# Input projections of heads 2 to 7 as block products, seven for eight

## The chip, the cores and the metric

The kernel runs on one core of a Trainium2 chip. The metric is the device time of one execution in microseconds (us). Five engines work side by side, each in the order of its own queue: TensorE (PE: matmuls, with its weight loads, PEld), VectorE (DVE: elementwise work and sums), ScalarE (ACT: functions, copies, rounding), GpSimd (POOL) and SyncE (SP), whose queue here issues the DMA transfers. They wait for one another by semaphores. SBUF is the memory that the engines work in, PSUM the one that TensorE writes its sums to.

## The reference

One step of a one-layer encoder for 512 prompt frames and 32 frames of a running stream, 544 tokens of 2048 features. The part that matters here is the first projection and the recurrent heads that read it:

```python
def token_mixer(x, s0, ...):
    proj = x @ w_in                                  # 544 x 2048 by 2048 x 4928
    hq, hf, hi, hg, cq, ckv, kr = jnp.split(proj, SPLITS, axis=-1)
    f = lb + (1.0 - lb) * jax.nn.sigmoid(hf)
    o_h, s_new = hgrn2_recurrence(heads(hq), heads(1.0 - f), heads(jnp.log(f)), heads(hi), s0, blk)
    o_h = rms_norm(o_h, hgrn_norm_g) * jax.nn.silu(hg)
    ...                                              # latent attention from cq, ckv, kr gives o_a
    out = jnp.concatenate([o_h, o_a], axis=-1) @ w_out
```

Each of the eight recurrent heads needs four blocks of 128 columns of the projection: q, f (forget gate), i (input) and g (output gate). Behind it stand the output projection, a layer norm and a feed-forward part with a convolution. All is float32.

## The kernel before

**Matmuls.** Features lie on the 128 partitions and tokens along the free axis. A float32 product is made from three matmuls in a faster rounded format (`mm3`, line 111): each operand is split into a rounded part and its remainder (`aH`, `aL` for the inputs; `wh`, `wl` for the weights), and rounded by rounded, rounded weight by remainder and remainder weight by rounded are summed in PSUM. ACT makes the rounded part of a weight (line 104), DVE the remainder (line 105). A matmul takes 128 features by 128 columns and one half of the tokens, 272, so one block of 128 columns costs 16 feature blocks x 3 x 2 halves = 96 matmuls.

**Heads.** `head_qf(h)` (line 338) projects q and f of a head, `head_ig(h)` (line 348) i and g: two blocks of 128 columns, 192 matmuls, from four weight pieces of 512 KB (`piece`: a load into one of three `raw` tiles, then the split into one of four pairs `wh`, `wl`). When a block is done, ACT copies it out of PSUM or applies the sigmoid, and DVE scales the forget gate (line 345) or multiplies the output gate (line 355).

**The recurrence** of a head runs beside the projections of the next: `levels(h)` (line 646) combines blocks of frames of doubled length in seven levels. In each, PE multiplies `Kp` and `Qp` (lines 674 to 679), then DVE updates `Qp` (line 680), POOL updates `Kp` (line 682) and DVE puts the result into a matrix (line 692). The next level's matmuls read the updated `Qp` and `Kp`. `finish(h)` (line 701) transposes, forms the states `S` and the output (lines 740, 742), normalises it (ACT squares at line 745, DVE sums at line 748, POOL takes the power at line 750, DVE multiplies at line 752), transposes it back (line 758) and multiplies by the gate (line 760). Outputs go to DRAM (`cat_dr`) for the output projection, whose first pieces (`out_first`, line 778) read them back into tiles `cx` and split them.

**Order.** `weave` (line 155) writes a chain of small steps between the pieces of a projection, at a given ratio; from that text a scheduler lays down the final queue of every engine. On the chip each queue is then worked off in order. The feed-forward part, written by hand, has its products in the form that the change brings to the heads.

Of the kernel before, what the change touches and what calls it, by code (L numbers as in the profile page):

```python
# [7 lines left out]
F32 = mybir.dt.float32  # L8
R = mybir.dt.float32r
# [6 lines left out]
P = 128  # L16
# [36 lines left out]
MANUAL = {mybir.EngineType.PE, mybir.EngineType.DVE, mybir.EngineType.Activation}  # L53
LEVELS = [1, 2, 4, 8, 16, 32, 64]


@with_exitstack
def tile_encoder_step(ctx, tc, xp, xs, w_in, w_kr, w_q_b, w_kv_b, w_out, w_up, w_gate, w_down, w_down2,
                      par_d, latp_d, krp_d, st_d, ident_d, cos_d, sin_d, amask_d, hmask_d,
                      y_d, lat_d, kr_d, stp_d, sts_d, conv_d):  # L60
    nc = tc.nc
# [46 lines left out]
    def piece(src, kc, ncols):  # L108
        return split_w(load_raw(src, kc, ncols), kc, ncols)
# [68 lines left out]

    ALLK = list(range(KD))

    def in_pieces(c):
        return lambda kk: piece(w_in[kk, c], 4, 256)

    aH, aL = [], []

# [7 lines left out]
    with tc.tile_pool(name="p0", bufs=1) as p0, tc.tile_pool(name="ps0", bufs=4, space=PSUM) as ps0:  # L193
# [12 lines left out]
        def load_first(kk):  # L206
            for g in range(2):
                raws[kk, g] = p0.tile([P, 4, 256], F32, name="raw0", tag="raw0", bufs=1) if g else \
                    wp.tile([P, 1024], F32, name="raw", tag="raw", bufs=3).rearrange("p (k c) -> p k c", k=4)
                dma(raws[kk, g], w_in[kk, 16 + g].rearrange("p (k c) -> p k c", k=4))  # L210

        G.memset(xt[4], 0.0)
        load_x(0)
# [413 lines left out]
        return cH[k], cL[k]  # L627


    with tc.tile_pool(name="gp", bufs=1) as gp, tc.tile_pool(name="psg", bufs=1, space=PSUM) as psg:  # L630
        hm = gp.tile([P, T + 272 * 6], I32, name="hm")
        dma(hm, hmask_d)
# [3 lines left out]
        rec = {}  # L636
        kT = gp.tile([P, 5, P], F32, name="kT")
        G.memset(kT[:, 4], 0.0)

        def sw_tile():  # L640
            return psg.tile([P, 1024], F32, name="sw", tag="sw")
# [59 lines left out]
        def finish(h):  # L701
            v, gate = hi[h], hgate[h]
            Kp, Qp, tot, tots, at, s0 = rec[h]
            vT = gp.tile([P, 5, P], F32, name="vT", tag="vT", bufs=1)
            for src, dst in ((Kp, kT), (v, vT)):
                tp = sw_tile()
                for j, (a, b) in enumerate(TOK):
                    PE.transpose(tp[:, j * P:(j + 1) * P], src[:, a:b], ident)  # L708
                if dst is kT:
                    A.activation(kT[:, :4].rearrange("p j c -> p (j c)"), tp[:, :512], AF.Copy)  # L710
                    A.activation(kT[96:128, 4], tp[96:128, 512:640], AF.Copy)
                else:
                    A.activation(dst.rearrange("p j c -> p (j c)"), tp[:, :640], AF.Copy)
                yield
            yield
            ss = s1_tile()
            for c in range(4):
                PE.matmul(ss[:, c * P:(c + 1) * P], kT[:, c], vT[:, c], start=True, stop=True)  # L718
            S = [None]
            for c in range(4):  # L720
                sc = gp.tile([P, P], F32, name="S", tag="S", bufs=5)
                if c == 0:
                    V.tensor_copy(sc, ss[:, 0:P])
# [7 lines left out]
            s1o = gp.tile([P, P], F32, name="s1o", tag="s1o", bufs=2)  # L731
            V.scalar_tensor_tensor(out=s1o, in0=s0, scalar=tots[:, 16:17], in1=ss[:, :P], op0=ALU.mult, op1=ALU.add)
            dma(sts_d[h], s1o)
            yield
            yield
            ops_ = sw_tile()
            for c, (ta, tb) in enumerate(TOK):
                cs = slice(c * P, (c + 1) * P)
                st = S[c] if c < 4 else s0
                PE.matmul(ops_[:, cs], at[:, ta:tb], vT[:, c], start=True, stop=c == 0)  # L740
                if c:
                    PE.matmul(ops_[:, cs], Qp[:, ta:tb], st, start=False, stop=True)  # L742
            o3 = ops_[:, :640].rearrange("p (c v) -> p c v", c=5)
            sq = gp.tile([P, 5, P], F32, name="sqg", tag="sqg", bufs=1)
            A.activation(sq, o3, AF.Square)
            r0 = gp.tile([P, 5], F32, name="r0", tag="r0", bufs=2)
            r1 = gp.tile([P, 5], F32, name="r1", tag="r1", bufs=2)
            V.reduce_sum(out=r0, in_=sq, axis=AX.X)
            V.tensor_scalar(out=r0, in0=r0, scalar1=1.0 / P, scalar2=RMS_EPS, op0=ALU.mult, op1=ALU.add)
            G.tensor_tensor(out=r1, in0=r0, in1=nhalf, op=ALU.pow)  # L750
            on = gp.tile([P, 5, P], F32, name="on", tag="on", bufs=1)
            V.tensor_tensor(out=on, in0=o3, in1=r1[:, :, None].to_broadcast([P, 5, P]), op=ALU.mult)
# [6 lines left out]
            o = gp.tile([P, T], F32, name="og", tag="og", bufs=2)  # L759
# [12 lines left out]
        for h in range(2, HEADS):  # L772
            weave([head_ig(h)], [levels(h)], 0.6)
            if h < HEADS - 1:
                weave([head_qf(h + 1)], [finish(h)], 0.7)
        wo_tiles = [main_tile(), main_tile()]

        def out_first():
            for kk in range(4):
                for k in CAT_ORDER[4 * kk:4 * kk + 4]:  # L780
                    if k != HEADS - 1:
                        cx = gp.tile([P, T], F32, name="cx", tag="cx", bufs=4)
                        dma(cx, cat_dr[k // 2][:, k % 2, :])
                        cH[k], cL[k] = split_act(cx)
            fin = finish(HEADS - 1)
            ks = CAT_ORDER
            for kk in range(4):
                wh, wl = out_piece(ks[kk * 4] // 4, 0)
                if kk == 3:
                    run(fin)  # L790
                for t, ps in enumerate(wo_tiles):
                    for k in range(4):
                        kg = ks[kk * 4 + k]
                        mm3(both(ps), (wh[:, k], wl[:, k]), (t * P, t * P + P), cact(kg),
                            kk == 0 and k == 0, kk == 3 and k == 3)
                        if k % 2 and kk < 3:
                            next(fin, None)
# [124 lines left out]
    hid_dr = dram.tile([P, NF - FD, T], F32, name="hd", tag="hd")  # L922

    ORDER = ("11", "s1", "s2", "s4", "s3", "12", "22")
    STORED = ("11", "12", "s1", "s2", "s3", "22", "s4")
    home, x1_op = {}, {}

# [1051 lines left out]
def _arrays(i):  # L1982
# [16 lines left out]
    w_main = np.concatenate([w_h, w_in[:, 4096:4864]], axis=1)  # L1999
# [10 lines left out]
    def striped(w):  # L2010
# [2 lines left out]
        return w.reshape(c // 512, 2, 2, P, 2 * NS * P)  # L2013

    arrs = [("xp", i["x_prompt"][0]), ("xs", i["x_sample"][0]), ("w_in", pieces(w_main, 4, 256)),
            ("w_kr", pieces(w_in[:, 4864:], 8, 64)[:, 0]), ("w_q_b", pieces(i["w_q_b"][0], 2, 384)),
            ("w_kv_b", pieces(i["w_kv_b"][0], 2, 512)), ("w_out", pieces(i["w_out"][0], 4, 256)),
            ("w_up", quads(i["w_ffn_up"][0])), ("w_gate", quads(i["w_ffn_gate"][0])),
# [30 lines left out]
```

## Time and profile before

| what | us |
|---|---|
| median of three timed runs (2419.14 to 2421.63) | 2420.24 |
| the profiled execution, its own time | 2417.4 |
| its span, first to last instruction | 2415.6 |
| up to the end of head 0's projections | 302 |
| projections of head 1 | 75 |
| projections of heads 2 to 7 | 364 |
| output projection and norm | 222 |
| feed-forward part: products up and gate, then down | 1278 |
| rest | 174 |

The stretches are read off the starts of instructions on the timeline. In the profile, the busy time of an engine counts its instructions, and overlapping matmuls count once; a group of instructions shows busy time, mean length of one, and the idle time just before them with what ended it; the chain of work that ended last is followed back from the last instruction. What a wait is put down to is inferred from semaphores.

### The profile page before, as it was taken

How to read it: one execution, taken by the hardware profiler on the slowest of the kernel's cores; microseconds unless marked ns; L12 is line 12 of the kernel's file. 1: busy time of each engine (PE TensorE's matmuls, PEld its weight loads, DVE VectorE, ACT ScalarE, POOL GpSimd, SP SyncE). 2: the span in 40 equal slices, each digit the busy share in tenths (PEclk: the TensorE clock that was granted, in tenths of full speed). 3: DMA queues.
4: the chain of work that ended last, by engine and by line, in shares of the span. 5: the costliest groups of instructions: out<-in, count | busy, mean ns of one | idle time of the engine just before them, and what ended most of it. 6: DMA issues, size and time to landing. Idle time of an engine off the chain costs nothing.

```text
span 2415.6 us, 44603 instructions
## 1 busy us (share of the span) xinstructions
PE 2365.5 (98%) x18750; PEld 2343.0 (97%) x18750; DVE 1666.5 (69%) x2263; ACT 980.0 (41%) x1487; POOL 181.6 (8%) x219
## 2 busy tenths in 40 slices
PE   7999999999999999999999999999999999999997
PEld 7999899999999998989999999999999999999996
DVE  7445544434345456889888888888777888888566
ACT  4244422222223224655555555555445433333234
POOL 4010020111111120000000000000000100000023
PEclk9999999999999999999999999999999999999998
DMA  7232132222235244536353534435243874642422
GB/s 238 89 94 71 61 103 86 78 79 78 79 92 192 88 123 150 178 119 203 109 194 110 178 130 143 165 115 192 88 126 120 344 298 139 234 134 88 121 66 75
DMA packets 123848, 324.29 MB, mean 134 GB/s; under 512 B 11008, under 2 KB 57856, under 8 KB 119040
## 3 DMA queue, kind: packets, MB, share of 16 engines
q1 hardware_dynamic: 114384, 277.99, 35.3%
q0 software_dynamic: 5040, 39.00, 4.1%
q10 hardware_dynamic: 4224, 4.46, 0.5%
q8 instruction: 147, 2.41, 0.4%
q14 instruction: 53, 0.43, 0.1%
HBM read 266.09 MB, written 53.92 MB: 132 GB/s over the span
## 4 chain that ended last, share of the span: by engine, by line
PE 80%; DVE 3%; ACT 1%; issue 1%; ACTq 0%; DVEq 0%
PE main L1025 20%; PE main L116 20%; PE acc L1025 16%; PE main L1053 8%; PE acc L1053 6%; PE acc L116 6%; PE s L676 1%; DVE wl L977 1%; PE sw L740 0%; PE sw L708 0%; ACT zb L1145 0%; ACT wh L976 0%; PE sw L742 0%; PE s L718 0%; PE sw L659 0%
## 5 line engine op out<-in xcount | busy, mean ns | idle before, releaser
L976 ACT ACTIVATE wh<-raw 128x1024 fp32r<-128x1024 f32 x340 | 359.9, 1059 | 414.0 <-DVE raw L969 133.7
L977 DVE TENSOR_TENSOR wl<-raw,wh 128x1024 fp32r<-128x1024 f32 x340 | 415.7, 1223 | 133.5 <-ACT wh L976 132.6
L116 PE MATMUL main<-aH,wh 128*128 128x272 f32 (+2 forms) x1536 | 348.5, 296 | 0.2 <-ACT x L262 0.2
L116 PE MATMUL main<-aL,wh 128*128 128x272 f32 (+2 forms) x1536 | 337.3, 289 | 3.7 <-POOL aL L264 3.7
L116 PE MATMUL main<-aH,wl 128*128 128x272 f32 (+2 forms) x1536 | 337.7, 289 | 0.0
L105 DVE TENSOR_TENSOR wl<-raw,wh 128x1024 fp32r<-128x1024 f32 (+2 forms) x128 | 149.7, 1171 | 236.1 <-ACT wh L104 231.3
L104 ACT ACTIVATE wh<-raw 128x1024 fp32r<-128x1024 f32 (+2 forms) x128 | 126.3, 991 | 364.5 <-PE main L116 284.2
L1025 PE MATMUL main<-op,wh 128*128 128x272 f32 x1408 | 265.6, 288 | 0.0
L1025 PE MATMUL acc<-ops,wh 128*128 128x272 f32 x1344 | 255.7, 289 | 4.2 <-DVE ops L1106 4.2
L116 PEld LDWEIGHTS main<-aL,wh 128*128 128x128 f32 x1536 | 249.9, 189 | 4.4 <-POOL aL L264 4.4
L1025 PE MATMUL main<-ops,wh 128*128 128x272 f32 x1344 | 254.1, 287 | 0.0
L116 PEld LDWEIGHTS main<-aH,wh 128*128 128x128 f32 x1536 | 248.6, 190 | 2.0 <-issue 0.5
L116 PEld LDWEIGHTS main<-aH,wl 128*128 128x128 f32 x1536 | 249.1, 190 | 0.0
L1025 PEld LDWEIGHTS main<-op,wh 128*128 128x128 f32 x1408 | 221.0, 188 | 0.0
L1025 PEld LDWEIGHTS acc<-ops,wh 128*128 128x128 f32 x1344 | 212.3, 189 | 4.5 <-DVE ops L1106 4.5
L1025 PEld LDWEIGHTS main<-ops,wh 128*128 128x128 f32 x1344 | 211.0, 188 | 0.0
L1025 PE MATMUL main<-op,wl 128*128 128x272 f32 x704 | 203.1, 289 | 0.9 <-DVE wl L977 0.9
L1025 PE MATMUL acc<-ops,wl 128*128 128x272 f32 x672 | 194.4, 289 | 0.0
L1025 PE MATMUL main<-ops,wl 128*128 128x272 f32 x672 | 193.8, 288 | 0.2 <-DVE wl L977 0.2
L1025 PE MATMUL acc<-op,wh 128*128 128x272 f32 x832 | 158.9, 289 | 1.6 <-DVE eg L1249 1.6
L976 ACT ACTIVATE wh<-rawl 128x1024 fp32r<-128x1024 f32 x93 | 98.5, 1059 | 105.9 <-DVE rawl L969 41.8
L969 DVE TENSOR_TENSOR raw<-raw,raw 128x1024 f32<-128x1024 f32 x114 | 139.2, 1221 | 1.7 <-DMA raw<-in_w_up 0.2
(395 smaller groups left out, 4865.7 us busy)
## 6 DMA issues: line engine op xcount, KB each, us to landing
raw<-in_w_in SPq DMA_DIRECT2D x76, 512.0 KB, 3.6
raw<-in_w_up SPq DMA_DIRECT2D x72, 512.0 KB, 4.6
raw<-in_w_gate SPq DMA_DIRECT2D x72, 512.0 KB, 4.2
raw<-in_w_down SPq DMA_DIRECT2D x71, 512.0 KB, 3.8
raw<-in_w_out SPq DMA_DIRECT2D x40, 512.0 KB, 3.5
opd<-ohl SPq DMA_DIRECT2D x16, 1088.0 KB, 5.5
ops<-opd POOLq DMA_DIRECT2D x16, 1088.0 KB, 9.2
opd<-ohl SPq DMA_DIRECT2D x16, 816.0 KB, 6.4
```

The costliest lines, as they stand in the source:

```text
L104: A.activation(dst(hv), src(rv), AF.Copy)
L105: V.tensor_tensor(out=dst(lv), in0=src(rv), in1=dst(hv).bitcast(F32), op=ALU.subtract)
L116: PE.matmul(ps, ww[:, wcols[0]:wcols[1]], aa[:, hs[j]], start=first and i == 0, stop=last and i == 2, skip_group_check=True)
L676: PE.matmul(ps[:, j * 64:(j + 1) * 64], Kp[:, a:b], Qv[:, j * bt:(j + 1) * bt, 1, :], start=True, stop=True)
L969: V.tensor_tensor(out=out, in0=a, in1=b, op=ALU.subtract)
L976: A.activation(wh, src, AF.Copy)
L977: V.tensor_tensor(out=wl, in0=src, in1=wh.bitcast(F32), op=ALU.subtract)
L1025: PE.matmul(ps, ww[:, k * P:(k + 1) * P], aa, start=self.first and k == 0 and i == 0, stop=k == n - 1 and i == 2, skip_group_check=True)
L1053: PE.matmul(banks[:, 512 * u:512 * u + NI], ww[:, (u * n + k) * P:(u * n + k + 1) * P], aa, start=self.first and k == 0 and i == 0, stop=k ...
```

## The change

The projections of heads 2 to 7 (twelve groups: q with f, i with g) are made as a two by two block product: inputs in two halves of 1024 features, tokens in two halves of 272, outputs in the two blocks of 128 columns. Eight block products become seven, on sums and differences of blocks, in the order `11, s1, s2, s4, s3, 12, 22`. Each product is 8 feature blocks x 3 = 24 matmuls of 272 columns. The weights of a group come as four blocks of 512 KB (two halves of inputs by two of outputs). DVE forms differences of them in place (`form`), and each of the seven is split as before (`split`). The sums of inputs `s1`, `s2`, `s4` are formed once, beside head 1, from the stored inputs (`h0_dr`), into tiles of their own; the fourth, `s3`, goes to DRAM and from there over the first 1024 features of the second half of tokens in `aH` and `aL`, which nothing reads after head 1. Products accumulate in two PSUM halves; four results are copied out by ACT, three added by DVE. Head 0 and 1 and the attention's projections stay as they were.

```diff
+N_PLAIN = 4
...
+        sums = {n: [gp.tile([P, 2, 4, NI], R, name=f"{n}{i}", tag=f"{n}{i}") for i in range(2)] for n in ("s1", "s2", "s4")}
...
+        def load_sums():
+            for k in range(HK):
+                for dst, kg, j in (("s1", k, 1), ("s2", k, 0), ("s4", HK + k, 0)):
+                    dma(part(dst, k, 1).bitcast(F32), h0_dr[kg][:, H_[j]])
+                dma(part("s1", k, 0).bitcast(F32), h0_dr[HK + k][:, H_[1]])
+
+        def sums_of_inputs():
+            load_sums()
+            for k in range(HK):
...
+                V.tensor_tensor(out=a, in0=t0, in1=t1, op=ALU.subtract)
+                V.tensor_tensor(out=b, in0=t1, in1=t1b, op=ALU.add)
+                V.tensor_tensor(out=c, in0=b, in1=t0, op=ALU.subtract)
+                two(a, s3[:, 0], s3[:, 1])
+                dma(s3_dr[k], s3.bitcast(F32))
+                yield
+                V.tensor_tensor(out=a, in0=t0b, in1=c, op=ALU.subtract)
+                for n, x in (("s1", b), ("s2", c), ("s4", a)):
+                    two(x, part(n, k, 0), part(n, k, 1))
+                yield
+
+        def place_s3():
+            for k in range(HK):
+                for i, t in enumerate((aH, aL)):
+                    dma(t[k][:, H_[1]].bitcast(F32), s3_dr[k][:, i])
+
+        class Divided:
...
+            def form(self, name):
+                if name == "11":
+                    for key in ("11", "12", "22", "21"):
+                        self.load(key)
+                r = self.raw
+                for n, out, a, b in (("s1", "11", "12", "11"), ("s2", "11", "22", "11"), ("s3", "12", "22", "12"),
+                                     ("22", "21", "21", "11")):
+                    if n == name:
+                        V.tensor_tensor(out=r[out], in0=r[a], in1=r[b], op=ALU.subtract)
...
+        def divided(c, a, b, after):
+            ps = main_tile()
+            x, y = ps[:, :NI], ps[:, 512:512 + NI]
+            t0, t1 = H_
+            for i, name in enumerate(ORDER):
+                n = 7 * (c - N_PLAIN) + i
+                ready(n + 2)
+                wh, wl = split_of.pop(n)
+                out = x if name in ("11", "s2", "s3", "22") else y
+                for k in range(HK):
+                    oh, ol = operand(name, k)
+                    for q, (ww, aa) in enumerate(((wh, oh), (wh, ol), (wl, oh))):
+                        PE.matmul(out, ww[:, k * P:(k + 1) * P], aa, ...)
+                    if k % 4 == 3:
+                        yield
+                kept = {"11": a[:, t0], "s1": b[:, t1], "s2": b[:, t0], "22": a[:, t1]}.get(name)
+                if kept is not None:
+                    A.activation(kept, out, AF.Copy)
+                else:
+                    z = {"s4": b[:, t0], "s3": b[:, t1], "12": a[:, t0]}[name]
+                    V.tensor_tensor(out=z, in0=z, in1=out, op=ALU.add)
+                    if name != "12":
+                        after(z)
...
-                sc = gp.tile([P, P], F32, name="S", tag="S", bufs=5)
+                sc = gp.tile([P, P], F32, name="S", tag="S", bufs=4)
...
-            on = gp.tile([P, 5, P], F32, name="on", tag="on", bufs=1)
+            on = sq
...
-        weave([head_qf(1)], [levels(0)], 0.6)
-        weave([head_ig(1)], [levels(1), finish(0)], 1.2)
-        weave([head_qf(2)], [finish(1)], 0.7)
+        of_inputs = sums_of_inputs()
+        weave([beside(head_qf(1), of_inputs, 2)], [levels(0)], 0.6)
+        weave([beside(head_ig(1), of_inputs, 2)], [levels(1), finish(0)], 1.2)
+        run(of_inputs)
+        place_s3()
+        weave([divided_qf(2)], [finish(1)], 0.8)
         for h in range(2, HEADS):
-            weave([head_ig(h)], [levels(h)], 0.6)
+            weave([divided_ig(h)], [levels(h)], 0.7)
             if h < HEADS - 1:
-                weave([head_qf(h + 1)], [finish(h)], 0.7)
+                weave([divided_qf(h + 1)], [finish(h)], 0.8)
...
-                for k in CAT_ORDER[4 * kk:4 * kk + 4]:
+                cx = gp.tile([P, 4, T], F32, name="cx", tag=("s10", "s11", "s20", "s21")[kk])
+                for i, k in enumerate(CAT_ORDER[4 * kk:4 * kk + 4]):
                     if k != HEADS - 1:
-                        cx = gp.tile([P, T], F32, name="cx", tag="cx", bufs=4)
-                        dma(cx, cat_dr[k // 2][:, k % 2, :])
-                        cH[k], cL[k] = split_act(cx)
+                        dma(cx[:, i], cat_dr[k // 2][:, k % 2, :])
+                        cH[k], cL[k] = split_act(cx[:, i])
```

What it does to the queues shows at three places of a head. First TensorE beside the recurrence of head 3, before: `s` is the result of a level (line 676 for prompt blocks, 679 for the stream), `main` the projection.

```order
L676 MATMUL s_5100<-Qp,Kp 128x64 x4
L679 MATMUL s_5100<-Qp,Kp 128x16
L116 MATMUL main<-aH,wh 128x272 x2
L116 MATMUL main<-aL,wh 128x272 x2
L116 MATMUL main<-aH,wl 128x272 x2
L116 MATMUL main<-aH,wh 128x272 x2
L116 MATMUL main<-aL,wh 128x272 x2
L116 MATMUL main<-aH,wl 128x272 x2
L676 MATMUL s_5123<-Qp,Kp 128x64 x4
L679 MATMUL s_5123<-Qp,Kp 128x16
```

Twelve matmuls of the projection stand between two levels. The same levels of head 3 on TensorE in the changed kernel (lines 824 and 827 are the levels, 753 the products; `s_3428` and `s_3429` are sums of inputs), here from the second level to the third:

```order
L753 MATMUL main<-s_3428,wh 128x272 x2
L753 MATMUL main<-s_3428,wl 128x272
L824 MATMUL s_5288<-Qp,Kp 128x64 x4
L827 MATMUL s_5288<-Qp,Kp 128x16
L824 MATMUL s_5311<-Qp,Kp 128x64 x3
L753 MATMUL main<-s_3429,wh 128x272 x2
L753 MATMUL main<-s_3429,wl 128x272
```

The third level (`s_5311`) follows the second (`s_5288`) at once; its last part comes 24 matmuls later and is followed at once by the fourth (`s_5352`):

```order
L753 MATMUL main<-s_3430,wh 128x272 x2
L753 MATMUL main<-s_3430,wl 128x272
L824 MATMUL s_5311<-Qp,Kp 128x64
L827 MATMUL s_5311<-Qp,Kp 128x16
L824 MATMUL s_5352<-Qp,Kp 128x64 x4
L827 MATMUL s_5352<-Qp,Kp 128x16
```

From the fifth level on, 24 matmuls of a product stand between two levels. The third place is VectorE's queue while `finish` normalises an output (748 to 752) and multiplies it by the gate (760); before:

```order
L105 TENSOR_TENSOR wl<-raw,wh 128x1024
L748 TENSOR_REDUCE r_4878<-sqg 128x5
L749 TENSOR_SCALAR r_4878<-r_4878 128x5
L752 TENSOR_TENSOR on<-sw,r_4879 128x640
L105 TENSOR_TENSOR wl<-raw,wh 128x1024
L760 SCALAR_TENSOR_TENSOR og<-sw,par,hproj 128x512
```

And in the changed kernel (718 is a remainder of weights, 711 a difference of weight blocks, 762 an addition out of PSUM, 774 the scaling of half a forget gate, 896 to 900 the normalisation):

```order
L762 TENSOR_TENSOR hproj<-hproj,main 128x272
L718 TENSOR_TENSOR wl<-raw,wh 128x1024
L896 TENSOR_REDUCE r_5068<-sqg 128x5
L774 TENSOR_SCALAR hproj<-hproj,oml,lb 128x272
L897 TENSOR_SCALAR r_5068<-r_5068 128x5
L711 TENSOR_TENSOR raw<-raw 128x1024
L900 TENSOR_TENSOR sqg<-sw,r_5069 128x640
```

One scaling and one difference now stand between the steps of the normalisation, and an addition that waits for the product `s4` ahead of them. The transposes of the normalised output on TensorE (line 906) stand 34 matmuls behind the output's last one, where 36 stood before.

More of the change, by code (lines that the diff above doesn't have):

```diff
@@ L627, in cact @@
         return cH[k], cL[k]
+    ORDER = ("11", "s1", "s2", "s4", "s3", "12", "22")
+    s3_dr = [dram.tile([P, 2, NI], F32, name=f"s3d{k}", tag=f"s3d{k}") for k in range(HK)]
     with tc.tile_pool(name="gp", bufs=1) as gp, tc.tile_pool(name="psg", bufs=1, space=PSUM) as psg:
@@ L638, in tile_encoder_step, with part @@
         G.memset(kT[:, 4], 0.0)
+        sums = {n: [gp.tile([P, 2, 4, NI], R, name=f"{n}{i}", tag=f"{n}{i}") for i in range(2)] for n in ("s1", "s2", "s4")}
+        def part(n, k, i):
+            return sums[n][k // 4][:, i, k % 4]
+        def load_sums():
[3 more added lines that the diff above has]
+                dma(part("s1", k, 0).bitcast(F32), h0_dr[HK + k][:, H_[1]])
@@ new lines, in sums_of_inputs, with two @@
+        def sums_of_inputs():
+            load_sums()
+            for k in range(HK):
+                t1, t0, t1b, t0b = (part(n, k, i).bitcast(F32) for n, i in (("s1", 1), ("s2", 1), ("s1", 0), ("s4", 1)))
+                t = gp.tile([P, HK * P], F32, name="s_f", tag="raw21")
+                a, b, c = (t[:, i * NI:(i + 1) * NI] for i in range(3))
+                s3 = gp.tile([P, 2, NI], R, name="s3", tag="sg")
+                def two(x, h, l):
+                    A.activation(h, x, AF.Copy)
+                    V.tensor_tensor(out=l, in0=x, in1=h.bitcast(F32), op=ALU.subtract)
+                V.tensor_tensor(out=a, in0=t0, in1=t1, op=ALU.subtract)
[8 more added lines that the diff above has]
+                yield
@@ new lines, in operand, with ready @@
+        def operand(name, k):
+            if name in sums:
+                return part(name, k, 0), part(name, k, 1)
+            kg, j = {"11": (k, 0), "s3": (k, 1), "12": (HK + k, 0), "22": (HK + k, 1)}[name]
+            return aH[kg][:, H_[j]], aL[kg][:, H_[j]]
+        products = [(g, name) for g in map(Divided, range(N_PLAIN, 2 * HEADS)) for name in ORDER]
+        split_of, begun = {}, []
+        def ready(n):
+            if not begun:
+                products[0][0].form(products[0][1])
+            while len(begun) <= min(n, len(products) - 1):
+                m = len(begun)
+                split_of[m] = products[m][0].split(products[m][1])
+                begun.append(m)
+                if m + 1 < len(products):
+                    products[m + 1][0].form(products[m + 1][1])
@@ new lines, in divided @@
+        def divided(c, a, b, after):
[10 more added lines that the diff above has]
+                    for q, (ww, aa) in enumerate(((wh, oh), (wh, ol), (wl, oh))):
+                        PE.matmul(out, ww[:, k * P:(k + 1) * P], aa, start=name in ("11", "s1", "12") and k == 0 and q == 0,
+                                  stop=k == HK - 1 and q == 2, skip_group_check=True)
+                    if k % 4 == 3:
[3 more added lines that the diff above has]
+                    A.activation(kept, out, AF.Copy)
+                else:
+                    z = {"s4": b[:, t0], "s3": b[:, t1], "12": a[:, t0]}[name]
+                    V.tensor_tensor(out=z, in0=z, in1=out, op=ALU.add)
+                    if name != "12":
+                        after(z)
@@ new lines, in proj_tile, with divided_qf, forget, divided_ig @@
+        def proj_tile():
+            return hp.tile([P, T], F32, name="hproj", tag="hproj")
+        def divided_qf(h):
+            q, f = proj_tile(), proj_tile()
+            def forget(z):
+                A.activation(z, z, AF.Sigmoid)
+                V.tensor_scalar(out=z, in0=z, scalar1=oml[:, h:h + 1], scalar2=lb[:, h:h + 1], op0=ALU.mult, op1=ALU.add)
+            yield from divided(2 * h, q, f, forget)
+            hq[h], hf[h] = q, f
+        def divided_ig(h):
+            i, g = proj_tile(), proj_tile()
+            def gate(z):
+                e = gp.tile([P, 2, NI], F32, name="sg", tag="sg")[:, 0]
+                A.activation(e, z, AF.Sigmoid)
+                V.tensor_tensor(out=z, in0=z, in1=e, op=ALU.mult)
+            yield from divided(2 * h + 1, i, g, gate)
+            hi[h], hgate[h] = i, g
@@ L767, in finish, with beside @@
                 cH[h], cL[h] = split_act(o)
-        weave([head_qf(1)], [levels(0)], 0.6)
-        weave([head_ig(1)], [levels(1), finish(0)], 1.2)
-        weave([head_qf(2)], [finish(1)], 0.7)
+        def beside(main, side, every):
+            for n, _ in enumerate(main):
+                if n % every == every - 1:
+                    next(side, None)
+                yield
+        of_inputs = sums_of_inputs()
[4 more added lines that the diff above has]
+        weave([divided_qf(2)], [finish(1)], 0.8)
         for h in range(2, HEADS):
-            weave([head_ig(h)], [levels(h)], 0.6)
+            weave([divided_ig(h)], [levels(h)], 0.7)
             if h < HEADS - 1:
-                weave([head_qf(h + 1)], [finish(h)], 0.7)
+                weave([divided_qf(h + 1)], [finish(h)], 0.8)
         wo_tiles = [main_tile(), main_tile()]
```

30 lines of the change are left out of this document (23 added, 7 removed).

## The prediction

> **What bounds the kernel now.** I read the page first: the busy time of the engines and, further down, the chain of work that ended last.
>
> ```profile
> span 2415.6 us, 44603 instructions
> PE 2365.5 (98%) x18750; PEld 2343.0 (97%) x18750; DVE 1666.5 (69%) x2263; ACT 980.0 (41%) x1487; POOL 181.6 (8%) x219
> ...
> PE 80%; DVE 3%; ACT 1%; issue 1%; ACTq 0%; DVEq 0%
> ```
>
> TensorE (PE) is busy for 98% of the span and carries the chain; VectorE (DVE) is busy for 69% and is hardly on it. Busy PE time alone doesn't say that PE is at its limit, so the stretches come next. The busy time by windows has, for each stretch, its length, then PE, weight load, DVE, ScalarE (ACT) and GpSimd (POOL), the granted clock, and the DMA share.
>
> ```profile
> 302.00:377.05 75.05, 74.62 (x616) 73.62 (x616) 33.72 (x67) 15.69 (x20) 15.43 (x18) 1.00 0.30 99
> 406.00:467.30 61.30, 61.30 (x505) 61.09 (x504) 24.58 (x43) 13.40 (x18) 7.33 (x8) 1.00 0.24 77
> 1000.00:1900.00 900.00, 893.74 (x7114) 892.68 (x7113) 765.37 (x822) 472.74 (x734) 4.05 (x7) 1.00 0.45 150
> ```
>
> The first stretch is head 1 (with the recurrence of head 0 beside it), the second one of the heads 2 to 7, the third the feed-forward part. In the second PE has no hole at all at full clock and DVE works 24.6 of 61.3 us: this stage is bound by the number of matmuls. The third already runs seven products for eight, with DVE at 85%, and PE still loses under 1%: a warning and an encouragement. A head's length is taken from the instruction that scales the forget gate, head 2 and head 7, on the timeline:
>
> ```profile
> 408.08 0.56 DVE L345 TENSOR_SCALAR hproj<-hproj,oml,lb 128x544 f32<-128x544 f32 x1
> 714.45 0.56 DVE L345 TENSOR_SCALAR hproj<-hproj,oml,lb 128x544 f32<-128x544 f32 x1
> ```
>
> Five heads lie between, so 306.37 / 5 = 61.3 us each.
>
> **What is removed.** Each of the twelve groups (q with forget, input with gate, of heads 2 to 7) has 192 matmuls of 272 columns before and 7 x 24 = 168 after: 288 fewer. The mean of 288 ns that the groups show for one is latency, since they overlap; what counts is the spacing, which a long unbroken piece of the chain gives (start, length, count):
>
> ```profile
> 1098.95 12.03 PE main L1025 x96
> ```
>
> 12.03 / 96 = 0.1253 us, so **288 x 0.1253 = 36.1 us** leave PE, and a head's PE work falls from 61.3 to 55.3 us. [...] The matmul rows of the new PE order do count 2016 for these groups, so that the change does what it says isn't in doubt.
>
> **What DVE gets.** Durations of one, from the groups of instructions (busy, mean ns):
>
> ```profile
> L105 DVE TENSOR_TENSOR wl<-raw,wh 128x1024 fp32r<-128x1024 f32 x112 | 139.8, 1248 | 220.3 <-ACT wh L104 215.7 <-PE tp L256 3.9
> L969 DVE TENSOR_TENSOR raw<-raw,raw 128x1024 f32<-128x1024 f32 x114 | 139.2, 1221 | 1.7 <-DMA raw<-in_w_up 0.2
> L1842 DVE TENSOR_TENSOR y<-y,main 128x272 f32<-128x272 f32 x21 | 8.2, 430 | 1.2 <-PE main L116 0.9 <-PE main L1835 0.2
> L1305 DVE TENSOR_TENSOR eg<-eg 128x272 f32<-128x272 f32 x64 | 25.6, 438 | 1.1
> ```
>
> Per head: 8 remainders of weights go (10.0 us), 14 come (17.5), 8 differences of weight blocks come (9.8), 6 additions out of PSUM come (2.6). DVE's 24.6 becomes 44.5 of about 55 us, 81%. That fits, as it does in the feed-forward part; what decides is where it waits. ACT adds six roundings and a few copies to 13.4 us and stays under half. So I take the adding itself as hidden, and price the places where the new order leaves PE nothing to do.
>
> **Levels without cover.** A level of the recurrence is a few small matmuls; POOL and DVE then update the operands that the next level reads. Before, 6 to 24 projection matmuls stand between two levels (the rows in the section on the change). From the timeline of PE, DVE and POOL (start, duration):
>
> ```profile
> 481.07 1.00 PE L676 MATMUL s<-Qp,Kp 128*128 128x64 f32 x8
> 481.91 0.35 PE L679 MATMUL s<-Qp,Kp 128*128 128x16 f32 x2
> 482.10 0.50 PE L116 MATMUL main<-aH,wh 128*128 128x272 f32 x2
> 482.29 0.44 DVE L680 TENSOR_TENSOR Qp<-Qp,tot 128x272 f32<-128x272 f32 x1 [1.26 <-PE s L679]
> 482.39 0.91 POOL L682 TENSOR_TENSOR Kp<-Kp,tot 128x272 f32<-128x272 f32 x1 [1.62 <-PE s L679]
> ```
>
> PE goes on at 482.10; POOL has the operand ready at 482.39 + 0.91 = 483.30. A bare pair of levels thus costs 483.30 - 482.10 = 1.20 us. The new order has two of them in every input-gate group (third level behind second, fourth behind third), and one pair with 8 matmuls (1.00 us) between, which lacks 0.20: 2.6 us a head, **6 x 2.6 = 15.6 us**. Below, the bound is nothing, if PE is then waiting for weights anyway; above, DVE's update stands behind one remainder and one difference (2.47 us) and the pair costs up to 2.5 more, 15 in all.
>
> **The normalised output.** After the recurrence's output PE needs ACT's squares, DVE's sum, POOL's power and DVE's product before it can transpose:
>
> ```profile
> 370.32 0.39 PE L742 MATMUL sw<-s,Qp 128*128 128x128 f32 x2
> 370.46 0.50 PE L116 MATMUL main<-aH,wh 128*128 128x272 f32 x2
> 370.75 0.70 ACT L745 ACTIVATE sqg<-sw 128x640 f32<-128x640 f32 x1 [1.16 <-PE sw L742]
> 371.48 0.82 DVE L748 TENSOR_REDUCE r<-sqg 128x5 f32<-128x640 f32 x1 [0.63 <-ACT sqg L745]
> 372.34 0.17 DVE L749 TENSOR_SCALAR r<-r 128x5 f32<-128x5 f32 x1
> 373.79 0.83 DVE L752 TENSOR_TENSOR on<-sw,r 128x640 f32<-128x640 f32 x1 [1.28 <-POOL r L750]
> ```
>
> From 370.46 to 374.62 are 4.16 us. Before, 36 matmuls (4.51) cover them; now 24 + 10 (4.26), and a remainder, a scaling and a difference are queued on DVE between these steps. The difference falls into the wait for POOL (1.28), most of the remainder into ACT's square. Between 0 and the 2.8 us of the three I take **0.6 a head, 3.6 in all**.
>
> **Sums of inputs beside head 1.** 64 DVE instructions of 272 columns x 0.438 = 28.0 us and 3 early differences (3.7) come to the 33.7 that DVE works in those 75.05: 65.4, room for 9.6. ACT's 32 roundings fit beside 15.7. If none of the new work fell into waits that DVE has there now (75.05 - 33.7 = 41.3 idle, of which some 24 behind PE, ACT and POOL), it would need 65.4 + 24 = 89, 14 too many; if all does, nothing. The new order puts the sums between the level updates, just where the waits are, so I take **3 us**. The 32 loads, 8 stores and 16 loads that put a sum in place of old inputs are SP's:
>
> ```profile
> 309.11 0.33 SPq L95 DMA_DIRECT2D raw<-in_w_in  x1
> raw<-in_w_in SPq DMA_DIRECT2D x76, 512.0 KB, 3.6
> ```
>
> At 0.33 each the 32 take 10.6 us of SP, and 4.5 MB meet a DMA share of 0.30. The weight load behind them is for the third piece of head 1's second group, needed some 40 us later. The 16 loads wait for PE's last reading of those inputs, and stores and the fourth block of head 2 are queued behind them; that block is the sixth product's, 5 x 24 x 0.1253 = 15 us after the group begins, and lands 3.6 us after its issue. Hidden; if the cover went, a landing or two, inside the bound above.
>
> **The output projection's first pieces.** Its fifteen inputs are now loaded into the tiles of the sums and split after the last group's third product, instead of earlier:
>
> ```profile
> L175 DVE TENSOR_TENSOR aL<-cx,aH x15: 711/726/837, 716.9 to 744.8; 128x544 fp32r<-128x544 f32 x15
> ```
>
> 15 x 0.726 = 10.9 us of DVE come later, beside about 28 us of PE work; the first of them is waited for. Bounds 0 and 10.9, and as the order has only one pair ahead of need, **1 us**. The fewer buffers for states and outputs are refilled a head later (61 us) than their stores, which costs nothing.
>
> **Sum.** -36.1 + 15.6 + 3.6 + 3 + 1 = **-12.9 us** against the profiled execution's own 2417.4 (span 2415.6 and 1.8 around it): 2404.5. The median of the three timed runs is 2420.24, 2.84 above it, so the forecast is **2407**.
>
> **Rivals.** (a) *Only the bare level pairs cost.* The rest is filled: -36.1 + 15.6 = -20.5, so 2400. For it: DVE idles 37 of 61.3 us now; the feed-forward part loses next to nothing. Against: POOL's step can't be shortened.
>
> (b) *POOL's update finds DVE in a long instruction with two inputs.* The same instruction with and without POOL running:
>
> ```profile
> 475.59 0.90 POOL L682 TENSOR_TENSOR Kp<-Kp,hproj 128x272 f32<-128x272 f32 x1 [16.26 <-PE s L679]
> 476.05 0.73 DVE L680 TENSOR_TENSOR Qp<-Qp,hproj 128x272 f32<-128x272 f32 x1
> L680 DVE TENSOR_TENSOR Qp<-Qp,hproj x8: 442/734/747, 314.7 to 721.2; 128x272 f32<-128x272 f32 x8
> ```
>
> It takes 0.73 when POOL started first and 0.442 at best, so one waits for the other. If POOL loses, a bare pair pays up to a remainder more: 12 x 1.25 = 15.0 us, so 2404.5 + 15.0 + 2.84 = **2422**, no change. For it: DVE is four fifths busy, mostly with such instructions. Against: at both bare pairs POOL is released with DVE waiting for the same PE event. [...]
>
> (c) *DVE's waits stay waits.* DVE takes its queue in order; a level update that waits for PE holds up the remainders behind it, PE then waits for those. The waits now, heads 3 to 7 (total us, times, longest):
>
> ```profile
> DVE Qp L680 <- PE s L679: 29.8, 18, 2.8
> DVE Qp L680 <- PE s L676: 8.1, 5, 1.6
> DVE Qp L680 <- PE s L674: 8.4, 5, 1.7
> DVE S L723 <- PE s L718: 8.9, 5, 1.8
> DVE r L748 <- ACT sqg L745: 10.6, 5, 2.1
> DVE on L752 <- POOL r L750: 6.4, 5, 1.3
> ```
>
> 72.2 us in a window of 285, that is 4.65 heads, so 15.5 a head. Unfilled, a head takes 44.5 + 15.5 = 60.0: -1.3 x 6 = -7.8, and with the upper ends of head 1 (14) and of the output pieces (10.9) the change loses 17.1: **2437**. It decides against PE once over 58.5 - 44.5 = 14 us a head stay unfilled (58.5 being 55.3 + 3.2 of holes). Against: in the new order weights are split two to four products ahead.
>
> **Chances and range.** Forecast 0.45, (a) 0.20, (b) 0.17, (c) 0.18. The likeliest case has 2400 to 2414 by itself. With level pairs that cost half (7.8 less than (a)) the low side is near 2392; I set 2390. (c) reaches beyond 2437 and half of it is kept: 2432. A measurement tells about 0.2% (4.8 us) from no change: faster 0.63 (the forecast's upper tail taken off), same 0.19, slower 0.18.
>
> **What would show it.** PE's waits in heads 2 to 7 should be for POOL's operand update at the second and third of a head's level steps, 1.2 us each and about 2.6 a head; a head should last 58 to 59 us from forget gate to forget gate, DVE busy near 44; head 1 should be some 3 us longer than 75. If PE instead waits for weight remainders, (c) is right; if the bare pairs cost 2 us or more with POOL starting late, (b); if there is no wait at the pairs, the order's holes were filled and my largest loss is wrong.

## The result: slower by 0.9%

| kernel | median us (timed runs) | ratio to before, 95% interval |
|---|---|---|
| before | 2420.26 (2419.14 to 2421.63) | |
| changed | 2441.69 (2439.59 to 2446.31) | 1.0091 [1.0073, 1.0108] |

The change takes 288 matmuls away and makes the kernel 21.4 us longer, where I had forecast 2407 and a range up to 2432. The page of the changed kernel, its busy times and the chain that ended last:

```profile
span 2437.8 us, 44485 instructions
PE 2356.3 (97%) x18462; PEld 2324.2 (95%) x18462; DVE 1801.7 (74%) x2459; ACT 1037.5 (43%) x1603; POOL 188.6 (8%) x219
...
PE 64%; DVE 3%; ACT 1%; issue 1%; ACTq 0%; DVEq 0%
```

TensorE (PE) has fewer instructions and nearly the same busy time in a longer span. The busy times by windows, cut at the scaling of the forget gate in heads 2 to 7 (length, PE, weight load, DVE, ACT, POOL, granted clock, DMA share, GB/s), show where:

```profile
401.20:463.30 62.10, 57.30 (x457) 55.66 (x456) 42.96 (x67) 21.04 (x31) 8.45 (x8) 1.00 0.24 76
463.30:528.40 65.10, 60.32 (x457) 58.68 (x456) 42.91 (x66) 21.04 (x31) 8.45 (x8) 0.95 0.23 73
528.40:592.00 63.60, 58.81 (x457) 57.16 (x456) 42.95 (x66) 21.11 (x31) 8.45 (x8) 0.97 0.24 74
592.00:654.20 62.20, 57.41 (x458) 55.78 (x458) 43.05 (x67) 21.04 (x31) 8.46 (x8) 1.00 0.25 76
654.20:719.30 65.10, 60.30 (x457) 58.66 (x456) 42.93 (x67) 21.04 (x31) 8.44 (x8) 0.95 0.23 72
```

A head took 61.3 us before and was to take 58 to 59. It takes 62.1 where the clock is full and 65.1 where it is not, and the clock had been 1.00 in all these heads before. DVE works 42.9 us a head, close to the 44.5 that I had worked out. PE's waits in these five heads (total us, times, longest):

```profile
PE s L824 <- POOL Kp L830: 6.4, 10, 1.1
PE sw L856 <- ACT kT L859: 6.2, 5, 1.2
PE s L824 <- DVE attnT L840: 5.8, 5, 1.2
PE sw L906 <- DVE sqg L900: 5.5, 5, 1.1
```

None is for a weight remainder. Each head has two long waits at the level pairs (the third row, and half of the first row's ten times; the other half are 0.2 us ahead of the second level, which has 8 projection matmuls before it), one between the two transposes (line 856) and one for the normalised output. The timeline around a bare pair of head 2:

```profile
420.04 0.34 PE L827 MATMUL s<-Qp,Kp 128*128 128x16 f32 x2
420.42 0.44 DVE L828 TENSOR_TENSOR Qp<-Qp,tot 128x272 f32<-128x272 f32 x1 [1.45 <-PE s L827]
420.52 0.97 POOL L830 TENSOR_TENSOR Kp<-Kp,tot 128x272 f32<-128x272 f32 x1 [1.48 <-PE s L827]
421.54 0.88 PE L824 MATMUL s<-Qp,Kp 128*128 128x64 f32 x6 [1.16 <-DVE attnT L840]
```

PE ends the second level; DVE and POOL start their updates within 0.1 us of each other, POOL takes 0.97 us (before, 0.69 to 0.99 for this update), and PE goes on 1.16 us later by the row's own note. The note names DVE's copy (line 840), but the third level reads only `Qp` and `Kp`, and POOL's update of `Kp` ends at 420.52 + 0.97 = 421.49, 0.05 ahead of PE's start. The same place in head 3, cut where the granted clock changes, at 484.9, 488.3, 491.7 and 495.2 us:

```profile
481.50:484.90 3.40, 2.24 (x20) 2.14 (x19) 2.37 (x4) 0.81 (x2) 0.97 (x1) 1.00 0.00 0
484.90:488.30 3.40, 3.40 (x17) 3.40 (x16) 1.32 (x2) 0.00 (x0) 0.00 (x0) 0.50 0.19 41
488.30:491.70 3.40, 2.31 (x21) 2.22 (x20) 1.95 (x4) 1.34 (x2) 0.90 (x1) 1.00 0.28 113
491.70:495.20 3.50, 3.50 (x18) 3.50 (x17) 1.51 (x6) 0.00 (x0) 0.87 (x1) 0.51 0.52 157
```

In the first and the third stretch PE works 2.2 to 2.3 of 3.4 us, much of it on levels of 64 columns; in the second and fourth PE has no hole, and half the clock (0.50 and 0.51). Between 463 and 800 us the granted clock has eight such stretches, seven in heads 3 to 7 and one at 795 in the output projection; before it had none from 45 to 965 us.

So two things were to be explained: why the queue has these holes, and whether DVE's load, which rival (c) blamed and whose time came out, has a part in it.

### The profile page after: what moved, and what is told of

Its sections match the earlier page's. It is cut to its first block, busy times and chain, and to the rows that moved or that the text cites. A ratio compares the mean times of both kernels' runs of the same rounds, so it can differ in the third digit from the quotient of the medians.

```text
span 2437.8 us, 44485 instructions
## 1 busy us (share of the span) xinstructions
PE 2356.3 (97%) x18462; PEld 2324.2 (95%) x18462; DVE 1801.7 (74%) x2459; ACT 1037.5 (43%) x1603; POOL 188.6 (8%) x219
## 3 DMA queue, kind: packets, MB, share of 16 engines
q8 instruction: 145, 2.38, 0.4%
## 4 chain that ended last, share of the span: by engine, by line
PE 64%; DVE 3%; ACT 1%; issue 1%; ACTq 0%; DVEq 0%
PE main L1179 20%; PE acc L1179 16%; PE main L1207 8%; PE main L118 7%; PE acc L1207 6%; PE acc L118 5%; DVE wl L1131 1%; PE main L753 1%; ACT zb L1299 0%; ACT wh L1130 0%; DVE raw L1123 0%; DVE ops L1260 0%; DVE zb L1294 0%; DVE wl L107 0%; PE main L993 0%
## 5 line engine op out<-in xcount | busy, mean ns | idle before, releaser
L1130 ACT ACTIVATE wh<-raw 128x1024 fp32r<-128x1024 f32 x340 | 359.9, 1059 | 415.6 <-DVE raw L1123 133.2
L118 PE MATMUL main<-aH,wh 128*128 128x272 f32 (+2 forms) x768 | 183.5, 296 | 1.5 <-ACT x L267 1.5
L118 PE MATMUL main<-aL,wh 128*128 128x272 f32 (+2 forms) x768 | 180.2, 292 | 4.0 <-POOL aL L269 3.9
L118 PE MATMUL main<-aH,wl 128*128 128x272 f32 (+2 forms) x768 | 179.0, 291 | 0.0
L717 ACT ACTIVATE wh<-raw 128x1024 fp32r<-128x1024 f32 x84 | 88.9, 1059 | 193.0 <-PE main L753 85.5
L107 DVE TENSOR_TENSOR wl<-raw,wh 128x1024 fp32r<-128x1024 f32 (+2 forms) x80 | 89.8, 1127 | 103.8 <-ACT wh L106 98.7
L106 ACT ACTIVATE wh<-raw 128x1024 fp32r<-128x1024 f32 (+2 forms) x80 | 75.5, 950 | 147.8 <-PE acc L118 65.6
L1131 DVE TENSOR_TENSOR wl<-rawl,wh 128x1024 fp32r<-128x1024 f32 x93 | 113.8, 1223 | 32.7 <-ACT wh L1130 32.6
L118 PEld LDWEIGHTS main<-aL,wh 128*128 128x128 f32 x768 | 129.9, 191 | 4.9 <-POOL aL L269 4.9
```

What stands on the lines that cost most here:

```text
L106: A.activation(dst(hv), src(rv), AF.Copy)
L107: V.tensor_tensor(out=dst(lv), in0=src(rv), in1=dst(hv).bitcast(F32), op=ALU.subtract)
L118: PE.matmul(ps, ww[:, wcols[0]:wcols[1]], aa[:, hs[j]], start=first and i == 0, stop=last and i == 2, skip_group_check=True)
L717: A.activation(wh, self.raw[key], AF.Copy)
L1130: A.activation(wh, src, AF.Copy)
L1131: V.tensor_tensor(out=wl, in0=src, in1=wh.bitcast(F32), op=ALU.subtract)
```

## The experiments

**Theory 1**: holes in TensorE's own queue, and the half clock behind them. **Theory 2**: VectorE's load and its waits, rival (c). **Theory 3** came from the runs: what makes the scheduler leave the holes.

**no_differences.** The changed kernel with this left out:

```diff
                 for n, out, a, b in (("s1", "11", "12", "11"), ...):
-                    if n == name:
-                        V.tensor_tensor(out=r[out], in0=r[a], in1=r[b], op=ALU.subtract)
+                    pass
```

> The changed kernel without the differences of weight blocks (the seven products take the blocks as they were loaded, so that the outputs are not the reference's): 48 VectorE instructions of 1.22 us less, 9.8 us a head, with level pairs and transposes still bare in TensorE's queue. Theory 1: a head stays at 61 to 63 us where the clock is full, time within 8 us of the changed kernel. Theory 2: a head falls to about 60 us or below by what VectorE no longer has to do, and the time by 15 us or more.

2439.54 us in one run. Three heads of it by windows:

```profile
467.40:532.60 65.20, 60.60 (x458) 58.78 (x457) 34.02 (x59) 20.91 (x31) 7.55 (x8) 0.95 0.23 73
532.60:596.30 63.70, 59.09 (x457) 57.27 (x457) 34.01 (x59) 20.91 (x31) 7.55 (x8) 0.97 0.24 74
596.30:658.40 62.10, 57.49 (x457) 55.68 (x456) 33.95 (x59) 20.91 (x31) 7.55 (x8) 1.00 0.25 76
```

DVE's column falls from 42.9 to 34.0 us a head, and the heads last 65.2, 63.7 and 62.1 us as before this edit, at the same clocks. DVE's load doesn't set a head's length: theory 2 falls.

**sums_alone.** Heads 2 to 7 by `head_qf` and `head_ig` as before, `sums_of_inputs` kept:

```diff
-N_PLAIN = 4
+N_PLAIN = 16
...
-        place_s3()
-        weave([divided_qf(2)], [finish(1)], 0.8)
+        weave([head_qf(2)], [finish(1)], 0.7)
```

> Heads 2 to 7 projected as before, but the sums of inputs still loaded and formed beside head 1 and the output projection's inputs still read through the tiles of the sums (the sum that goes over old inputs is stored but not put there). Theory 1: head 1 costs 2 to 4 us more than before, the output projection's first pieces 0 to 5, time 2422 to 2429. Theory 2: VectorE's waits beside head 1 stay waits, head 1 costs 10 us or more, time 2430 or more.

2423.60 us in one run. The start of the first and third recurrence (head 0 and head 2) and a matmul of the output projection behind its first pieces, on the timelines of before and of this run:

```profile
306.51 0.44 DVE L653 TENSOR_SCALAR Kp<-hproj 128x544 f32<-128x544 f32 x1 [2.83 <-DMA catd<-o]
408.68 0.44 DVE L653 TENSOR_SCALAR Kp<-hproj 128x544 f32<-128x544 f32 x1
798.13 0.42 PE L116 MATMUL main<-aH,wh 128*128 128x272 f32 x2
```

```profile
307.05 0.45 DVE L801 TENSOR_SCALAR Kp<-hproj 128x544 f32<-128x544 f32 x1 [2.84 <-DMA catd<-o]
413.49 0.44 DVE L801 TENSOR_SCALAR Kp<-hproj 128x544 f32<-128x544 f32 x1
802.95 0.42 PE L118 MATMUL main<-aH,wh 128*128 128x272 f32 x2
```

The run is 0.54 us late at the first, 4.81 at the second and 4.82 at the third. Head 1 pays 4.3 us for the sums, just above the 2 to 4 expected; the heads behind it and the output projection's first pieces pay nothing.

**text_order.** Since the holes stand in the scheduler's order, the first cure was to write the order by hand, for three engines (PE, DVE, ACT):

```diff
+        with tc.manual_schedule(engines=MANUAL):
-        weave([divided_qf(2)], [finish(1)], 0.8)
+            weave([divided_qf(2)], [finish(1)], 0.8)
...
```

> The changed kernel with nothing altered but the order of heads 2 to 7: PE, DVE and ACT take the program's text as it is written, so that 12 or 24 projection matmuls (1.5 or 3.0 us) stand between any two levels of the recurrence, between the two transposes and behind the recurrence's output. Theory 1 (holes in TensorE's own queue, and the granted clock that falls to half behind them): a head falls from 62.1 to 65.2 us to 55.5 to 57.5, no stretch of heads 2 to 7 below clock 1.00, time 2390 to 2402. Theory 2 (VectorE's load and its waits, my rival c): VectorE works as much as before in the text's order, a head stays at 60 us or more with TensorE waiting for weight remainders, time 2425 or more.

2507.99 us, ratio 1.0368 [1.0350, 1.0385]: theory 1 is far off, and theory 2 has the time in its open end, but not the waits that it named. PE's waits in four heads:

```profile
PE main L753 <- DVE hproj L762: 39.4, 21, 4.3
PE main L753 <- ACT hproj L759: 13.5, 20, 1.4
PE main L753 <- ACT wh L717: 5.8, 4, 1.5
```

The level pairs are gone from the list. PE now waits at the beginning of a product for a *result* to be taken out of PSUM, by ACT (line 759) or DVE (line 762), and these stand in their queues behind splits of weights.

**text_bare_pairs** is text_order with both pairs bare again (a `yield` ends a step of a chain; without it the next level follows at once):

```diff
                 tot = nt
-                yield
+                if m not in (2, 4):
+                    yield
```

> The kernel of text_order with one difference: no step of the projection between second and third and between third and fourth level. Theory 1: two pairs of 1.2 us in each of six heads, 14.4 us more than text_order, and up to 1.7 us more for every 3.4 us stretch that gets half the clock behind them: 14 to 30 us more. Theory 2: the same time as text_order within 5 us, since VectorE's work is the same.

2529.35 us in one run, 21.4 more than text_order, inside the 14 to 30 of theory 1. The edit takes the step out of heads 0 and 1 too: 2.1 of the 21.4 are there when head 2's recurrence starts (423.94 us on the timeline for 421.87).

**text_order_pe.** As text_order, with `engines={mybir.EngineType.PE}`.

> As text_order, but only TensorE takes heads 2 to 7 in the order of the text (12 or 24 projection matmuls between any two levels, 12 between the transposes, 48 behind the recurrence's output); VectorE and ScalarE are ordered by the scheduler again, results out of PSUM ahead of weight splits. Theory 1 (holes in TensorE's own queue and the half clock behind them; what ruined text_order is that results out of PSUM stand behind splits on VectorE and ScalarE): a head of 55.5 to 57.5 us, clock 1.00 throughout heads 2 to 7, time 2388 to 2402. Theory 2 (any queue that keeps the seven products fed keeps TensorE waiting, at VectorE's 43 us a head): a head of 60 us or more, TensorE waiting for results out of PSUM or for weights, time 2425 or more.

2470.52 us, ratio 1.0207 [1.0190, 1.0224]: what theory 2 expected, in time and in waits, though no_differences had shown that less work on DVE doesn't help. So covering the levels can't be all, and the waits have to be read. Four heads by windows, and PE's waits in them:

```profile
471.80:749.00 277.20, 231.09 (x1822) 222.38 (x1822) 171.60 (x262) 84.17 (x125) 30.44 (x32) 1.00 0.22 68
```

```profile
PE main L753 <- ACT hproj L759: 29.9, 24, 1.7
PE main L753 <- DVE hproj L762: 16.2, 16, 1.2
```

All waits are at the beginning of products, 40 in four heads of 14 products. One of them on the timeline:

```profile
529.38 0.38 ACT L759 ACTIVATE hproj<-main 128x272 f32<-128x272 f32 x1
533.92 0.29 PE L753 MATMUL main<-s,wl 128*128 128x272 f32 x1
534.17 1.06 ACT L717 ACTIVATE wh<-raw 128x1024 fp32r<-128x1024 f32 x1 [4.41 <-DVE S L873]
535.13 0.38 ACT L759 ACTIVATE hproj<-main 128x272 f32<-128x272 f32 x1
535.56 0.51 PE L753 MATMUL main<-s,wh 128*128 128x272 f32 x2 [1.35 <-ACT hproj L759]
```

The product `s2` (half `x`) ends with the matmul of 533.92; ACT, which has a rounding first, copies its result at 535.13, and only then does PE go on with `s4`. But `s4` writes half `y`, whose own last result, of `s1`, was copied at 529.38. The first matmul of this product waits, 1.35 us, for the result of the product *just before*: `x` and `y` are two halves of one tile `ps`, and the order between the engines was kept by tile here (PE went on at 535.56), not by half, which was free from 529.38 + 0.38 = 529.76 on. This is theory 3. In the changed kernel these places aren't seen as waits, because the scheduler put other work there: level steps, transposes, the next group's first product. That is why the levels stand 24 matmuls apart and two at a time.

**two_tiles.** Nothing written by hand; the two halves come from two tiles, which change places from group to group, since seven is odd:

```diff
+        halves = []
         def divided(c, a, b, after):
-            ps = main_tile()
-            x, y = ps[:, :NI], ps[:, 512:512 + NI]
+            if not halves:
+                halves.extend([main_tile(), main_tile()])
+            x, y = halves[c % 2][:, :NI], halves[1 - c % 2][:, :NI]
```

> The changed kernel with the two halves that a group's products accumulate in taken from two PSUM tiles instead of the two halves of one; no order written by hand. In the queue the first matmul of a product then waits for the result of the product before the last, not of the last, and the scheduler itself puts 12 or 24 projection matmuls between any two levels. Theory 3 (the one PSUM tile makes every product wait for the result before it, about 1.5 us each; the scheduler puts level steps into these waits, which is why they stand bare; the rest is the half clock behind the holes): a head of 55.3 to 56.5 us, clock 1.00 in heads 2 to 7, time 2386 to 2396. Theory 2 (VectorE's 43 us a head and its waits): a head of 60 us or more, time 2415 or more.

**2390.12 us, ratio 0.9876 [0.9860, 0.9893]**: faster than both kernels. Four heads by windows:

```profile
453.40:675.40 222.00, 222.00 (x1822) 220.82 (x1821) 171.16 (x262) 84.67 (x125) 30.32 (x32) 1.00 0.28 85
```

A head lasts 222.0 / 4 = 55.5 us, PE has no hole, the clock is 1.00, and DVE works 42.8 us a head (171.16 / 4), as much as in the changed kernel. The same text, given to the same scheduler, now has 12 or 24 projection matmuls between any two levels, 12 between the transposes and 48 ahead of the normalised output's. In the heads that I laid side by side, that is block for block TensorE's order in text_order_pe, where a head took 277.20 / 4 = 69.3 us: the same queue with one tile and with two, so the gain is the tiles' and not the order's.

**two_tiles_bare and two_tiles_bare_filled.** What does a hole cost? The first takes two_tiles, PE in the text's order, and leaves out the `yield` behind the second and third level of heads 2 to 7. The second puts work into the two holes:

```diff
+                if m in (2, 4) and h >= 2:
+                    w = part("s1", 0, 0)
+                    for _ in range(8):
+                        PE.matmul(ps[:, 272:512], w[:, :P], w[:, :240], start=True, stop=True, ...)
```

> The kernel of two_tiles with TensorE's order as in the text and no projection step between second and third and third and fourth level of heads 2 to 7, so that only these two pairs are bare. Theory 1: 2.4 us a head (14.4 in all) by the waits for the operand updates, and behind them one or two stretches of 3.4 us at half clock in most heads, 1.0 to 1.7 us each: 15 to 30 us more than two_tiles. If bare pairs cost only their wait, 12 to 16 more; if they cost nothing, the same time.

> The kernel of two_tiles_bare with 8 matmuls of 240 columns, whose results nothing reads, in each of the two bare pairs (about 0.9 us of TensorE's work in a wait of 1.2). If the clock falls because TensorE streams too few columns in a stretch of 3.4 us: the waits stay in length, no stretch at half clock in heads 2 to 7, 12 to 16 us more than two_tiles and less than two_tiles_bare by what the half clock cost there. If the clock follows something else (the waits themselves): the same as two_tiles_bare or more.

2423.46 and 2405.40 us, one run each: 33.3 and 15.3 more than two_tiles, the first 3 above the range expected, the second inside its own. Four heads of the bare kernel by windows, then one hole cut into stretches, then its waits in heads 2 to 7:

```profile
459.90:705.50 245.60, 236.61 (x1822) 234.61 (x1821) 172.24 (x262) 83.72 (x125) 30.50 (x32) 0.94 0.25 77
476.70:480.10 3.40, 3.40 (x30) 3.38 (x28) 1.74 (x2) 1.34 (x2) 0.57 (x1) 1.00 0.29 117
480.10:483.50 3.40, 1.36 (x11) 1.19 (x10) 3.24 (x6) 0.00 (x0) 1.71 (x2) 1.00 0.00 0
483.50:490.30 6.80, 6.59 (x30) 6.59 (x31) 1.51 (x6) 1.34 (x2) 1.03 (x2) 0.50 0.28 80
```

```profile
PE s L827 <- DVE attnT L843: 7.0, 6, 1.2
PE s L827 <- POOL Kp L833: 6.5, 6, 1.1
```

And four heads of the filled one:

```profile
455.50:688.60 233.10, 231.21 (x1887) 228.59 (x1886) 174.95 (x262) 83.81 (x125) 29.79 (x32) 1.00 0.26 81
```

The bare kernel's waits are 13.5 us in all, 1.17 and 1.08 each, where I had put 1.20. But a stretch in which PE works 1.36 of 3.40 us is followed by 6.80 us at half clock, and a head takes 61.4 us. Filled, a head has the same pairs (second to third and third to fourth level start 2.35 and 2.57 us apart, bare 2.34 and 2.38), runs at clock 1.00 and takes 58.3: **2.8 us a head for the holes themselves, 3.1 more for the half clock behind them**. The levels of a pair are as far apart in both runs, within 0.2 us; the work of PE between them is not the same: with 8 matmuls that nothing reads in each hole the clock over four heads is 1.00 for 0.94, and the kernel 18 us faster.

## Why the prediction was wrong

**Removed matmuls: right.** 61.3 to 55.3 us a head was the forecast, and two_tiles has 55.5 without a hole: -34.8 in six heads for my -36.1.

**Adding on DVE is hidden: right.** 42.9 us a head for 44.5, and without the differences (8.9 of it) the heads are no shorter. Rival (c) gave 2437, close to the measured time by luck, for its mechanism isn't there: in the changed kernel PE waits for no remainder. In text_order it waits a little for the rounded part of weights (line 717), and that order is another.

**Rival (b): wrong.** At the bare pairs POOL starts 0.10 us behind DVE and takes 0.97.

**Levels without cover: the price right, the cause not seen.** 2.6 us a head, forecast; 12.2 us of waits in five heads are 2.4. I took the pairs as an accident of the order. They fill the ends of products, where a result must leave the shared PSUM tile. The two halves cut from one tile `ps` stand in the diff; I didn't ask what the first matmul of each product would wait for.

**The step that failed: "Levels without cover" and "The normalised output" as a list of all holes, priced at their length alone.** Two things were missing from the sum.

First, the list was short. The wait for the normalised output is 1.1 us a head (5.5 / 5), for 0.6. The second transpose waits 1.24 (6.2 / 5) for ACT to empty the one tile that both use; before, 12 matmuls stood there, now none, and I had no term for it. With the pairs' 2.44 that makes 4.78; a head at full clock lost 62.15 - 55.5 = 6.65. The other 1.9 stand in no row of waits. Laid beside a head of two_tiles, the starts of matmuls come another 0.1 to 0.2 us late at these same places, and a little behind each, which is about half of it; the rest is spread over shorter delays, and what makes them isn't shown.

Second, and not in the forecast in any form, the clock. 65.1 - 62.1 = 3.0 us for a head with two stretches at half clock, so 1.5 each and 10.5 for the seven in heads 3 to 7. The eighth follows matmuls of one column in the norm of the output projection (six records in 0.83 us at 794.68 us), which the kernel before has too (at 774.90), at clock 1.00; why it falls only here isn't shown, and its 1.5 is taken from the others. I had looked at the clock of before, which was full, and taken it as given.

| term, us | forecast | measured |
|---|---|---|
| matmuls removed | -36.1 | -34.8 (two_tiles) |
| holes in heads 2 to 7 at full clock | 15.6 + 3.6 | 6 x 6.65 = 39.9 |
| half clock behind them | none | 7 x 1.5 = 10.5 |
| half clock in the output projection | none | 1.5 |
| sums of inputs beside head 1 | 3 | 4.3 (sums_alone) |
| output projection's first pieces | 1 | 0 (sums_alone) |
| sum | -12.9 | +21.4 |

The sum agrees with the difference of the medians, 2441.69 - 2420.26 = 21.43, and without the output projection's 1.5 it agrees with the timelines: head 7's output is multiplied by its gate at 783.0 us, before at 763.2, 19.8 later. The holes' share and the clock's are worked out from the windows of the profiled run; their split was tried in two_tiles_bare and its filled twin, not in the changed kernel itself.

## What to carry to other kernels

Two accumulators that are meant to alternate belong in two PSUM tiles: in one, 40 of the 56 products of four heads waited for the result before them (46.1 us in text_order_pe), in two none did, and a scheduler hides that by spending the work that should have covered something else. Price a hole on TensorE at its length plus the half clock that may follow it: here 1.5 us a stretch, behind seven of the ten level pairs of heads 3 to 7 and behind neither of head 2. Where a hole can't be closed, work that nothing reads may be cheaper than none: 18 us in two_tiles_bare_filled. When an order looks odd, ask what its first instruction waits for before pricing it.

## What the runs showed of the hardware

In these runs the half clock came without an idle stretch. In the rows of head 3 above, 2.24 us of PE's work in 3.40 were followed by 3.40 us at clock 0.50, and 2.31 in 3.40 by 3.50 us at 0.51; no single wait of PE there is over 1.2 us. In two_tiles_bare 1.36 in 3.40 were followed by 6.80 us at 0.50.

It didn't come every time. At the bare pair of head 2, on the timeline above, PE works no more than that:

```profile
418.70:422.10 3.40, 2.05 (x17) 1.75 (x16) 1.95 (x5) 1.34 (x2) 1.31 (x2) 1.00 0.04 12
```

Yet the clock is 1.00 over the whole of that head, 401.20 to 463.30 us. In text_order_pe PE waits ten times a head, 1.2 us each (46.1 us in 40 waits), and the clock over four heads is 1.00; there a whole product, 24 matmuls of 272 columns, stands between one wait and the next. The levels, whose matmuls have 64 columns and fewer, stand around the holes that the half clock followed in heads 3 to 7. Why it followed seven of these ten pairs and not the other three, nor the two of head 2, isn't shown; some matmul records can be missing from a trace.
